# Three edits to a two-layer mixer on one core: four tiles for the rows of M, an interleaved start, and 512-column output products

## The chip, the cores and the metric

The kernel runs on one core of one Trainium2 chip, in one launch. The metric is the device time of one execution in microseconds (us). The engines are TensorE (PE, matrix products; PEld is its loading of weights), VectorE (DVE), ScalarE (ACT), GpSimd (POOL) and SyncE (SP), which issues the DMA transfers. Each engine works off its own list of instructions in order, and the order of each list is fixed when the program is built.

## The reference

Two layers, each on 512 latent tokens and 256 context tokens of 1024 channels (768 rows in all). A conditioning vector goes through the adaLN matrix (1024 x 3072) and gives a shift, a scale and a gate. Then, cut to what matters here:

```
h = rmsnorm(x, pre_g) * (1 + scale) + shift
s = split(h @ w_in)                    # 13,408 columns
ya = bidirectional RG-LRU(s)           # branch a
yb = bidirectional gated linear attention(s)   # branch b
yc = bidirectional Mamba-2 SSD(s)      # branch c, 32 heads of 64, state 128
pa, pb, pc = (ya*silu) @ w_pa, (norm(yb)*silu) @ w_pb, norm(yc*silu) @ w_pc
o  = (g0*pa + g1*pb + g2*pc) @ w_out
x  = x + gate * rmsnorm(o, post_g)
```

In branch c, within a chunk of tokens, y[t] = sum over s of cb[t,s] * exp(cum[t]-cum[s]) * x[s], plus the state's part, times exp(cum[t]), and then times the silu gate of z. cb times that exponential, masked, is the matrix M. The context runs through layer 0 in full; layer 1 needs only its states.

## The kernel before

**How products are made.** All of it is float32. A product a*b is three products of shorter numbers (fp32r): high part by high part, high by low, low by high. Whoever writes an operand for PE splits it: a copy into the high part (`hh`, `oh`, `wh`) and a subtraction for the low part (`hl`, `ol`, `wl`; L356 is the subtraction). Activations stand with channels on the partitions, as eight k tiles of 128 x 768.

**The order.** `Sched` is a list scheduler that runs when the program is built. Each piece of work is a stream (a Python generator) that yields operations, needs (events such as `("raw", 1)`: "weight tile 1 is loaded") and requests for a tile from a small ring (`Slots`). Among the streams that are free to go on, it takes the operation with the earliest modelled start; so any edit to a ring or a need can move everything behind it. Helpers emit all operations, so the profile's lines are mostly theirs: L410 matmul, L414 the half-width product with M, L419 transpose, L423 DMA, L332 activation, L373 two-operand DVE operation, L404 copy under a mask, L551 adaLN product.

**Weights.** An `Item` is 0.5 MB of weights and what is done with them. The `loader` brings items in order into a ring of two raw tiles (four in the ring that w_out has), the `splitter` splits each in two halves into `wh` and `wl` (four halves of 512 columns), and `main` runs the bodies in order. PSUM has two large tiles (`pp`, 2 x 512 columns) for projections and four small ones (`aux`).

**The start.** `start` loads eight adaLN blocks of 1 MB, ring of six, one after the other; the loads of x's six row tiles go between them (`x` stream i needs block i+1), and small parameters too. Blocks come as pairs (0 and 4, 1 and 5, ...): the pair gives shift and scale for two k tiles. `make_h_part` then makes the two k tiles for each of three pairs of row tiles (transposes, an affine step, a split). The first two items, the dt projection (96 columns) and the first x projection (128 columns), go through `acc_first`: row pairs 0 and 1 first over all k tiles, then row pair 2.

**M's rows.** `ssd_ms` makes one row of M (128 tokens x 4 heads) from two `rr` tiles: each is loaded by DMA (the cumulated sums, broadcast over the partitions), ACT adds a bias per head (four operations each), DVE merges the two under a mask, ACT takes the exponential, DVE multiplies by cb and sets the diagonal. The result stays in the first `rr` tile until PE has used it (L414, two products to a head pair); the second goes back at once. `ssd_ec` loads, per row, an `ec` tile of exp(cum); `ssd_scan` multiplies the state's products by it, adds, and `out` multiplies the sum by z's gate, which needs both z projections of the group (`gz`, L373), and only then gives the `ec` tile back. There are 80 rows.

**w_out.** Per pair of row tiles, `it_wout` runs four blocks of 256 columns by two halves of four k tiles; a body waits for both halves of its weights. A tail per block multiplies by the gate (`o`) and squares (`sq`); the last tail starts the closing normalisation, `post`.

Of the kernel before, what the change touches and what calls it, by code (L numbers as in the profile page):

```python
# [287 lines left out]
class Mixer(Sched):  # L288
# [288 lines left out]
    def ada_load(self, l, q, raws):  # L577
        for blk in ADA_BLOCKS:
            raw = yield from self.acquire(raws)
            yield from self.dma(raw, self.a["ada_w"][l][:, blk * 256:(blk + 1) * 256].rearrange("(k p) n -> p k n", p=P))  # L580
            self.first.append(raw)
            self.done.add(("adal", blk))
            yield from self.param_loads(l, q, 5)

# [22 lines left out]
    def loader(self, items):  # L607
        for i, it in enumerate(items):
            pieces, kk, nn = it.units
            if it.ring != "w":  # L610
                yield ("need", [("open", it.ring)])
            raw = yield from self.acquire(self.raws[it.ring])
            rv = raw[:, :kk * nn].rearrange("p (k n) -> p k n", k=kk)
            for c0, src in pieces:
                yield from self.dma(rv[:, :, c0:c0 + src.shape[1]], src.rearrange("(k p) n -> p k n", p=P))
            self.rawq.append((raw, rv))
            self.done.add(("raw", i))
# [71 lines left out]
    def acc_first(self, ps, us, l, rows=P):  # L689

        for pairs in ((0, 1), (2,)):
            for k in range(KT):
# [957 lines left out]
    def it_wout(self, S, pair, n, kh):  # L1650
        l = S.l
        early = n == 0 and pair == (0 if S.nc_ else 1)

        def tail(ps, n, o, x, ss):
            cs = slice(n * 256, (n + 1) * 256)
            for i in range(2):
                yield from self.tt(o[i][:, cs], ps[:, i, :256], S.gp[1 if pair == 0 else 0][:, cs], ALU.mult)
            for i in range(2):
                junk = yield from self.acquire(S.junk2_)
                yield from self.act(junk, ps[:, i, :256], AF.Square, accum=ss[i][:, n:n + 1])  # L1660
                self.free(junk)
            self.free(ps)
            if n == 3:
                self.spawn(("h", l + 1, pair), self.post(S, pair, o, x, ss), 1)
# [4 lines left out]
        def body(us):  # L1669
            if n == 0 and kh == 0:  # L1670
                o = yield from self.acquire(S.o_, 2)
                x = yield from self.acquire(S.x_in, 2)
                S.o = (o, x, [S.e_.tile([P, 4], F32, name=self.nm("ss")) for _ in range(2)])
                for i in range(2):
                    self.spawn(("xin", l, pair, i), load(i, x[i]), 2)
            if kh == 0:
                S.ops = yield from self.acquire(self.pp)
            yield ("need", [us.second])
            for i in range(2):
                out = S.ops[:, i, :256]  # L1680
                sl = slice((pair * 2 + i) * P, (pair * 2 + i + 1) * P)
                for kk in range(4):
                    k = kh * 4 + kk
                    h, lo = us.high(kk, 0, 256), us.low(kk, 0, 256)
                    yield from self.mm(out, S.mh[k][:, sl], h, k == 0, False)
                    yield from self.mm(out, S.mh[k][:, sl], lo, False, False)
                    yield from self.mm(out, S.ml[k][:, sl], h, False, k == KT - 1)
            if kh == 1:
                self.spawn(("wt", l, pair, n), tail(S.ops, n, *S.o), 0, [("gp", l), ("wt", l, pair, n - 1)] if n else [("gp", l)])
        need = [("pbr", l, 0, j) for j in range(8)] if (n, kh) == (0, 0) else []  # L1690
        return Item(("w", l, pair, n, kh), ([(0, self.a["w_out"][l][kh * 512:(kh + 1) * 512, n * 256:(n + 1) * 256])],
                                            4, 256), body, need, ring="w" if early else f"e{l}")

# [105 lines left out]
    def tail_items(self, S):  # L1799
        r = [self.it_wout(S, pr, n, kh) for pr in ((0, 1, 2) if S.nc_ else (1, 2))  # L1800
             for n in range(4) for kh in range(2)]
        return r

    def start(self, q, st, ip, src):
# [10 lines left out]
        def load(i):  # L1815
            yield from self.dma(xs[i], src(i))
            j = yield from self.acquire(junk)
            yield from self.norm_tile(ip, xs[i], j)
            self.free(j)
        for i in range(NCH):  # L1820
            self.spawn(("x", i), load(i), 0, [("adal", ADA_BLOCKS[1 + i])])
        self.alloc_h()
# [5 lines left out]
    def run(self):  # L1828
        a = self.a
        with self.tc.manual_schedule():  # L1830
# [15 lines left out]
            self.spawn(("par", 1), self.params(1, q1), 3, [("start",)])  # L1846
            self.spawn(("loader",), self.loader(items), 2, [("adaload",)])
            self.spawn(("splitter",), self.splitter(items), 2, urgent=lambda: self.ahead <= W_LOW)
# [4 lines left out]
class Layer:  # L1853
# [9 lines left out]
    def open_c(self):  # L1863
# [27 lines left out]
        self.sf_ = Slots(k, c, "sf", 2, [P, 256])  # L1891
        self.rr_ = Slots(k, c, "rr", 3, [P, 4, P])
        self.ec_ = Slots(k, c, "ec", 3, [P, 2, 2, P])

# [56 lines left out]
    def open_e(self):  # L1951
# [5 lines left out]
        self.junk_ = Slots(k, e, "junk", 1, [P, D])  # L1957
        self.junk2_ = Slots(k, e, "sq", 2, [P, 256])
        ring = f"e{self.l}"
# [48 lines left out]
```

## Time and profile before

| | |
|---|---|
| median of 3 runs | 2750.03 us (2747.54 to 2751.88) |
| the profiled execution | 2755.44 us, of it the span 2753.6 |
| mean granted clock of PE | 0.991 |
| busy: PE, DVE, ACT, POOL | 2667.7, 2104.9, 1222.8, 297.5 us |
| share of the span | 97%, 76%, 44%, 11% |
| DMA | 329.37 MB, 120 GB/s |

The span runs from the first instruction to the last; the profiled execution is 1.84 us longer. Busy times are sums over instructions. A timeline's line gives its start, its duration, the operation and how many ran in a row, and in brackets how long the engine had idled before and for whom. A clock of 1.00 is full speed, and 0.61 over a stretch is a mean over full and half speed.

### The profile page before, as it was taken

The numbers are of one execution on the slowest core, as the hardware profiler recorded it, in microseconds if no ns is written. First come the engines' busy times: TensorE is split into PE (matmuls) and PEld (weight loads), VectorE is DVE, ScalarE is ACT, GpSimd is POOL, SyncE is SP. The second block draws the span as 40 slices with busy tenths as digits, with TensorE's granted clock in tenths as the row PEclk, the third lists the DMA queues.
The fourth block names the chain that finished last, engine by engine and source line by source line (L and its number), as shares of the span: only waits on it lengthen the run. The fifth ranks groups of instructions, "written<-read, shape, count | busy, mean of one in ns | idle before, by whom it ended". The sixth has DMA issues, their size and how long they took to land. (4 is left out here: it accounts for less than half of the span.)

```text
span 2753.6 us, 42894 instructions
## 1 busy us (share of the span) xinstructions
PE 2667.7 (97%) x16294; PEld 2298.6 (83%) x16294; DVE 2104.9 (76%) x3990; ACT 1222.8 (44%) x2350; POOL 297.5 (11%) x398
## 2 busy tenths in 40 slices
PE   7999899999999999999999999999999999999898
PEld 5888788888889888888889987878888888888787
DVE  5788979898665653668956879999997766568987
ACT  4445555454413331326722555556453333246742
POOL 1021112122000000000000203122120000000000
PEclk9999899999999999999999999999999999999999
DMA  6353444435352222462155635344354532243255
GB/s 211 91 142 81 123 107 118 113 94 137 103 184 73 68 67 81 136 195 62 52 164 181 205 88 132 95 123 112 104 134 129 173 84 78 73 140 112 63 157 199
DMA packets 491966, 329.37 MB, mean 120 GB/s; under 512 B 19812, under 2 KB 466864, under 8 KB 491760
## 3 DMA queue, kind: packets, MB, share of 16 engines
q1 hardware_dynamic: 491760, 326.63, 42.1%
q8 instruction: 128, 2.10, 0.3%
q14 instruction: 78, 0.64, 0.1%
HBM read 294.12 MB, written 32.45 MB: 119 GB/s over the span
## 5 line engine op out<-in xcount | busy, mean ns | idle before, releaser
L410 PE MATMUL pp<-hh,wh 128*128 128x256 f32 (+2 forms) x2624 | 760.8, 352 | 13.0 <-DVE r L380 4.6
L410 PE MATMUL pp<-hl,wh 128*128 128x256 f32 (+2 forms) x2624 | 765.3, 353 | 0.2 <-DVE hl L356 0.2
L410 PE MATMUL pp<-hh,wl 128*128 128x256 f32 (+2 forms) x2624 | 763.0, 352 | 0.0
L410 PEld LDWEIGHTS pp<-hh,wh 128*128 128x128 f32 (+1 forms) x2624 | 487.3, 189 | 78.9 <-issue 9.6
L410 PEld LDWEIGHTS pp<-hh,wl 128*128 128x128 f32 (+1 forms) x2624 | 488.2, 189 | 60.0 <-issue 0.5
L410 PEld LDWEIGHTS pp<-hl,wh 128*128 128x128 f32 (+1 forms) x2624 | 487.4, 189 | 59.4 <-issue 1.2
L356 DVE TENSOR_TENSOR wl<-raw,wh 128x512 fp32r<-128x512 f32 (+1 forms) x628 | 442.6, 708 | 46.9 <-ACT wh L341 14.7
L342 DVE CAST wh<-raw 128x512 fp32r<-128x512 f32 (+1 forms) x364 | 159.4, 438 | 300.4 <-PE pp L410 282.6
L332 ACT ACTIVATE rr<-rr,tokp 128x128 f32<-128x128 f32 x640 | 202.7, 390 | 157.4 <-DMA rr<-cumd 156.9
L341 ACT CAST wh<-raw 128x512 fp32r<-128x512 f32 (+1 forms) x264 | 161.8, 617 | 233.2 <-PE pp L410 195.2
L375 POOL TENSOR_TENSOR xw<-xt,tokp 128x256 f32<-128x256 f32 x157 | 133.5, 850 | 529.3 <-DVE xwl L356 349.5
L332 ACT ACTIVATE r<-pp 128x768 f32<-128x768 f32 (+1 forms) x112 | 78.3, 700 | 187.1 <-PE pp L410 186.9
L410 PE MATMUL pp<-oh,wh 128*128 128x512 f32 (+1 forms) x384 | 119.3, 362 | 0.8 <-DVE gz L380 0.8
L410 PE MATMUL pp<-oh,wl 128*128 128x512 f32 (+1 forms) x384 | 117.9, 360 | 0.0
L410 PE MATMUL pp<-ol,wh 128*128 128x512 f32 (+1 forms) x384 | 117.9, 359 | 0.0
L410 PE MATMUL pp<-yh,wh 128*128 128x512 f32 (+1 forms) x384 | 116.1, 356 | 0.0
L410 PE MATMUL pp<-yh,wl 128*128 128x512 f32 (+1 forms) x384 | 115.6, 355 | 0.0
L410 PE MATMUL pp<-yl,wh 128*128 128x512 f32 (+1 forms) x384 | 115.4, 355 | 0.0
L410 PE MATMUL pp<-wh,hl 128*128 128x256 f32 x384 | 109.1, 284 | 0.0
L332 ACT ACT_TABLE_LOAD x79 | 101.4, 1283 | 17.1 <-PE pp L410 10.9
L410 PE MATMUL pp<-wl,hh 128*128 128x256 f32 x384 | 108.7, 283 | 0.0
L410 PE MATMUL pp<-wh,hh 128*128 128x256 f32 x384 | 108.7, 283 | 0.0
(275 smaller groups left out, 4887.9 us busy)
## 6 DMA issues: line engine op xcount, KB each, us to landing
raw<-in_w_in_dram SPq DMA_DIRECT2D x208, 512.0 KB
rr<-cumd SPq DMA_DIRECT2D x160, 256.0 KB
ec<-ecumd SPq DMA_DIRECT2D x160, 128.0 KB
raw<-in_w_out_dram SPq DMA_DIRECT2D x40, 512.0 KB
raw<-in_w_pc_dram SPq DMA_DIRECT2D x32, 512.0 KB
raw<-in_ada_w_dram SPq DMA_DIRECT2D x32, 512.0 KB
ada<-in_ada_w_dram SPq DMA_DIRECT2D x8, 1024.0 KB
raw<-in_w_pb_dram SPq DMA_DIRECT2D x16, 512.0 KB
```

The lines of the kernel that those rows point to most:

```text
L332: self.nc.scalar.activation(out, in_, func, **kw)
L341: yield from self.any_op([("ACT", self.acost(n, in_), lambda: self.nc.scalar.copy(out, in_)), ("DVE", self.vcost(n, in_, True), lambda: se ...
L342: ("DVE", self.vcost(n, in_, True), lambda: self.nc.vector.tensor_copy(out, in_))],
L356: ways = [("DVE", self.vcost(n, a), lambda: self.nc.vector.tensor_tensor(out, a, b, ALU.subtract))]
L375: ways.append(("POOL", self.gcost(n), lambda: self.nc.gpsimd.tensor_tensor(out, a, b, op)))
L410: lambda: self.nc.tensor.matmul(out, lhsT, rhs, start=start, stop=stop))
```

## The change

1. **The start.** The small parameters come after the second adaLN block, all six row tiles of x right behind them, then the weights of the first two items, and only then adaLN blocks three to eight. The third item's weights wait for the last block. `acc_first` in layer 0 goes k tile by k tile over the three row pairs, so a body can go on as each pair of blocks frees two k tiles.
2. **M's rows.** The ring `rr` has four tiles, and the ring `ec` two, each 2 KB a partition.
3. **w_out.** An item is two k tiles by 512 columns: 480 products of 512 columns instead of 960 of 256. The body begins with its first half, gives it back, and then waits for the second. Tails handle 512 columns.

```
@@ ada_load
-        for blk in ADA_BLOCKS:
+        for i, blk in enumerate(ADA_BLOCKS):
             raw = yield from self.acquire(raws)
+            if i == 2:
+                yield ("need", [("xl", t) for t in range(NCH)] + [("raw", 1)])
...
-            yield from self.param_loads(l, q, 5)
+            if i:
+                yield from self.param_loads(l, q)
@@ loader
+            if i == 2:
+                yield ("need", [("adaload",)])
@@ acc_first
+        if l == 0:
+            for k in range(KT):
+                for p in range(3):
+                    yield ("need", [("hk", l, p, k)] + ([us.second] if k >= KT // 2 else []))
+                    out = self.rows_of(ps[:rows, 1, :], l, p) if p else ps[:rows, 0, 512 - TC:]
+                    h, lo = us.high(k, 0, rows), us.low(k, 0, rows)
+                    for i, (w, x) in enumerate(((h, self.hh[k]), (h, self.hl[k]), (lo, self.hh[k]))):
+
+                        yield from self.mm(out, w, self.rows_of(x[:, TC:], l, p) if p else x[:, :TC],
+                                           k == 0 and i == 0 and p < 2, k == KT - 1 and i == 2 and p != 1)
+            return
@@ it_wout
-                yield from self.tt(o[i][:, cs], ps[:, i, :256], S.gp[1 if pair == 0 else 0][:, cs], ALU.mult)
+                yield from self.tt(o[i][:, cs], ps[:, i, :], S.gp[1 if pair == 0 else 0][:, cs], ALU.mult)
...
-            yield ("need", [us.second])
-            for i in range(2):
-                out = S.ops[:, i, :256]
-                sl = slice((pair * 2 + i) * P, (pair * 2 + i + 1) * P)
-                for kk in range(4):
-                    k = kh * 4 + kk
-                    h, lo = us.high(kk, 0, 256), us.low(kk, 0, 256)
+            for kk in range(2):
+                k = kh * 2 + kk
+                if kk:
+                    us.release(0)
+                    yield ("need", [us.second])
+                h, lo = us.high(kk, 0, 512), us.low(kk, 0, 512)
+                for i in range(2):
+                    out = S.ops[:, i, :]
+                    sl = slice((pair * 2 + i) * P, (pair * 2 + i + 1) * P)
                     yield from self.mm(out, S.mh[k][:, sl], h, k == 0, False)
                     yield from self.mm(out, S.mh[k][:, sl], lo, False, False)
                     yield from self.mm(out, S.ml[k][:, sl], h, False, k == KT - 1)
...
-        return Item(("w", l, pair, n, kh), ([(0, self.a["w_out"][l][kh * 512:(kh + 1) * 512, n * 256:(n + 1) * 256])],
-                                            4, 256), body, need, ring="w" if early else f"e{l}")
+        return Item(("w", l, pair, n, kh), ([(0, self.a["w_out"][l][kh * 256:(kh + 1) * 256, n * 512:(n + 1) * 512])],
+                                            2, 512), body, need, ring="w" if early else f"e{l}")
@@ start
             yield from self.dma(xs[i], src(i))
+            self.done.add(("xl", i))
...
-            self.spawn(("x", i), load(i), 0, [("adal", ADA_BLOCKS[1 + i])])
+            self.spawn(("x", i), load(i), 0, [("rows", 0)])
@@ run
-            self.spawn(("loader",), self.loader(items), 2, [("adaload",)])
+            self.spawn(("loader",), self.loader(items), 1, [("xl", t) for t in range(NCH)])
@@ open_c
-        self.rr_ = Slots(k, c, "rr", 3, [P, 4, P])
-        self.ec_ = Slots(k, c, "ec", 3, [P, 2, 2, P])
+        self.rr_ = Slots(k, c, "rr", 4, [P, 4, P])
+        self.ec_ = Slots(k, c, "ec", 2, [P, 2, 2, P])
```

Left out are a few lines that follow from it: the slices and counts in `it_wout` and `tail_items` (two blocks of 512 by four items), and the sizes of `sq` (512) and `ss` (2).

SP's list at the start, from the fourth adaLN block (`ada_174`) on, before:

```order
L423 DMA ada_174<-in_ada_w_dram 128x8x256
L423 DMA x_106<-in_x_dram 128x1024
L423 DMA ada_178<-in_ada_w_dram 128x8x256
L423 DMA x_107<-in_x_dram 128x1024
L423 DMA ada_181<-in_ada_w_dram 128x8x256
L423 DMA x_108<-in_x_dram 128x1024
L423 DMA ada_184<-in_ada_w_dram 128x8x256
L423 DMA x_109<-in_x_dram 128x1024
L423 DMA ada_197<-in_ada_w_dram 128x8x256
L423 DMA raw_202<-in_w_in_dram 128x8x64
L423 DMA raw_202<-in_w_in_dram 128x8x32
L423 DMA raw_208<-in_w_in_dram 128x8x128
```

and now, behind the row tile `x_107`:

```order
L423 DMA x_108<-in_x_dram 128x1024
L423 DMA x_109<-in_x_dram 128x1024
L423 DMA raw_178<-in_w_in_dram 128x8x64
L423 DMA raw_178<-in_w_in_dram 128x8x32
L423 DMA raw_188<-in_w_in_dram 128x8x128
L423 DMA ada_159<-in_ada_w_dram 128x8x256
L423 DMA ada_203<-in_ada_w_dram 128x8x256
L423 DMA ada_214<-in_ada_w_dram 128x8x256
L423 DMA ada_224<-in_ada_w_dram 128x8x256
L423 DMA ada_231<-in_ada_w_dram 128x8x256
L423 DMA ada_237<-in_ada_w_dram 128x8x256
```

The two items' weights (`raw`: 64 and 32 columns for dt, 128 for x) moved from behind the last adaLN block to ahead of the third (`ada_159`), and x's loads no longer alternate with the blocks.

PE's list at the start, at the last adaLN block's product (`ada_197`), before; `pp_459` is the dt projection, and its first product is the last row:

```order
L551 MATMUL aux_420<-ada_197,cfull 32x256 x8
L419 MATMUL aux_441<-ident,x_109 128x128
L419 MATMUL aux_442<-ident,x_109 128x128
L419 MATMUL aux_420<-ident,r_453 128x128 x2
L419 MATMUL aux_478<-ident,x_104 128x128
L419 MATMUL aux_478<-ident,x_105 128x128
L419 MATMUL aux_479<-ident,x_104 128x128
L419 MATMUL aux_479<-ident,x_105 128x128
L419 MATMUL aux_480<-ident,x_106 128x128
L419 MATMUL aux_480<-ident,x_107 128x128
L410 MATMUL pp_459<-hh_110,wh_209 96x256 x2
```

and now, around the product of the third block (`ada_203`), with `pp_313` the dt and `pp_322` the x projection, and the number behind `hh` counting the k tiles from 110:

```order
L419 MATMUL aux_192<-ident,r_347 128x128 x2
L410 MATMUL pp_313<-hh_110,wh_189 96x256
L410 MATMUL pp_322<-hh_110,wh_297 128x256
L410 MATMUL pp_313<-hl_118,wh_189 96x256
L410 MATMUL pp_313<-hh_110,wl_190 96x256
L410 MATMUL pp_313<-hh_111,wh_189 96x256
L410 MATMUL pp_322<-hl_118,wh_297 128x256
L410 MATMUL pp_322<-hh_110,wl_298 128x256
L410 MATMUL pp_322<-hh_111,wh_297 128x256
L551 MATMUL aux_346<-ada_203,cfull 32x256 x8
```

Products of both projections now stand among the adaLN blocks' own, with k tiles 110 and 111 ahead of the third block, where before the first product of a projection stood behind the last.

PE's list in layer 0 where group 0 of branch c ends (about 290 us before); `pp_3120` is a projection, `pp_3365` the first product with w_pc, `xt_2448` the x of group 1's first half, whose six rows of M are the 13th to 18th, before:

```order
L410 MATMUL pp_3120<-hh_117,wl_2974 128x512
L414 MATMUL aux_3231<-rr_3104,xt_2448 64x128 x4
L410 MATMUL aux_3232<-ct_2875,sb_2924 128x128 x2
L414 MATMUL aux_3285<-rr_3230,xt_2448 64x128 x4
L410 MATMUL aux_3286<-ct_2875,sf_3165 128x128 x2
L410 MATMUL aux_3319<-xwh_3310,btok_2872 128x256
L410 MATMUL aux_3319<-xwl_3311,btok_2872 128x256
L410 MATMUL aux_3319<-xwh_3310,btokl_2873 128x256
L414 MATMUL aux_3347<-rr_3284,xt_2448 64x128 x4
L410 MATMUL aux_3348<-ct_2875,sf_3210 128x128 x2
L410 MATMUL aux_3348<-ct_2875,sb_3124 128x128 x2
L410 MATMUL pp_3365<-oh_3244,wh_3045 128x256
```

and now, at the first of the same three rows of M (`xt_2563` is the same x):

```order
L410 MATMUL pp_3044<-hh_116,wl_2915 128x512
L414 MATMUL aux_3158<-rr_2970,xt_2563 64x128 x4
L410 MATMUL aux_3159<-ct_2801,sb_2840 128x128
L419 MATMUL aux_3136<-ident,r_3045 128x128 x4
L410 MATMUL aux_3159<-ct_2801,sb_2840 128x128
L410 MATMUL pp_3044<-hh_117,wh_2914 128x256
L410 MATMUL pp_3044<-hh_117,wh_2914 128x512
L410 MATMUL aux_3172<-xwh_3162,btok_2782 128x256
L410 MATMUL pp_3044<-hl_125,wh_2914 128x256
L410 MATMUL pp_3044<-hl_125,wh_2914 128x512
L410 MATMUL pp_3044<-hh_117,wl_2915 128x256
L410 MATMUL pp_3044<-hh_117,wl_2915 128x512
```

Before, three products with M stood in eight rows, with only small products between. Now the first of them is at row 1324 of PE's list and the next three at 1354, 1414 and 1441, with the rest of `pp_3044`, one more projection and the first two products with w_pc between them. On DVE's list the last low part of group 0 that w_pc needs (`ol`, from `gz`) is row 488, and was row 491. Over the whole program PE's list is 13,593 rows and was 14,027, DVE's 3891 and 3888, ACT's 1779 and 1809, POOL's 387 and 403.

## Rows read from the trace of the kernel before

**Rows 1.** Page, part 1: busy us (share of the span) x instructions
```profile
PE 2667.7 (97%) x16294; PEld 2298.6 (83%) x16294; DVE 2104.9 (76%) x3990; ACT 1222.8 (44%) x2350; POOL 297.5 (11%) x398
```

**Rows 2.** Page, part 2: busy tenths of PE in 40 slices
```profile
PE   7999899999999999999999999999999999999898
```

**Rows 3.** Windows: us, busy us of each engine, PE's clock, DMA share, GB/s
```profile
3.00:36.00 33.00, 20.10 (x138) 9.34 (x138) 13.35 (x50) 12.01 (x25) 4.53 (x11) 0.90 1.07 354
36.00:41.00 5.00, 3.29 (x39) 1.46 (x38) 4.70 (x13) 3.52 (x9) 0.95 (x2) 1.00 0.88 179
...
65.00:250.00 185.00, 183.69 (x1148) 157.84 (x1147) 147.33 (x295) 85.34 (x189) 28.39 (x35) 1.00 0.44 114
...
290.00:312.00 22.00, 11.06 (x57) 8.46 (x57) 21.58 (x38) 10.27 (x26) 2.40 (x4) 0.61 0.35 96
...
1495.00:1572.00 77.00, 73.59 (x606) 72.44 (x605) 66.11 (x128) 41.04 (x105) 13.40 (x18) 1.00 0.65 209
1760.00:1820.00 60.00, 57.41 (x310) 44.67 (x310) 57.17 (x115) 34.08 (x82) 15.01 (x18) 1.00 0.45 118
```

**Rows 4.** Timeline of PE, 0:110: start, us, line, operation [idle before <-releaser]
```profile
39.50 1.07 PE L551 MATMUL aux<-ada,cfull 128*32 128x256 f32 x16
...
42.73 0.48 PE L410 MATMUL pp<-hh,wh 128*96 128x256 f32 x2
...
64.55 0.28 PE L410 MATMUL pp<-hh,wl 128*128 128x256 f32 x1
```

**Rows 5.** Timeline of DVE, 39:46 us
```profile
44.35 0.54 DVE L350 TENSOR_SCALAR r<-aux,asc,mod 128x256 f32<-128x256 f32 x1
44.93 0.29 DVE L342 CAST hh<-r 128x256 fp32r<-128x256 f32 x1
45.26 0.42 DVE L356 TENSOR_TENSOR hl<-r,hh 128x256 fp32r<-128x256 f32 x1
```

**Rows 6.** Timeline of PE, 2689.7:2708.1, w_pa (512 columns), then w_out
```profile
2689.75 0.39 PE L410 MATMUL pp<-yh,wh 128*128 128x512 f32 x1
...
2694.96 0.39 PE L410 MATMUL pp<-yh,wl 128*128 128x512 f32 x1
...
2703.00 0.28 PE L410 MATMUL pp<-wh,ml 128*128 128x256 f32 x1
...
2707.80 0.28 PE L410 MATMUL pp<-wh,mh 128*128 128x256 f32 x1
```

**Rows 7.** Groups by form, whole run, then 1495:1572: busy, mean ns | idle, releaser
```profile
L410 PE MATMUL pp<-wl,mh 128*128 128x256 f32 x320 | 91.8, 287 | 4.3 <-DVE wl L356 4.3
...
L410 PE MATMUL pp<-wl,mh 128*128 128x256 f32 x191 | 55.1, 289 | 3.4 <-DVE wl L356 3.4
```

**Rows 8.** Groups by form, whole run: the tails of PSUM pieces
```profile
L373 DVE TENSOR_TENSOR ec<-aux,ec 128x512 f32<-128x512 f32 x64 | 43.9, 686 | 18.2 <-PE aux L410 17.9
...
L332 ACT ACTIVATE r<-pp 128x512 f32<-128x512 f32 x56 | 33.1, 592 | 63.8 <-PE pp L410 63.8
...
L373 DVE TENSOR_TENSOR o<-pp,gp 128x256 f32<-128x256 f32 x40 | 15.2, 417 | 4.1 <-PE pp L410 4.1
...
L332 ACT ACTIVATE sq<-pp 128x256 f32<-128x256 f32 x40 | 15.0, 380 | 20.4 <-DVE o L373 20.4
```

**Rows 9.** Timeline of PE, 255:330 us: products with M's rows
```profile
298.60 1.12 PE L414 MATMUL aux<-rr,xt 128*64 128x128 f32 x8 [5.44 <-DVE rr L404]
...
307.08 1.12 PE L414 MATMUL aux<-rr,xt 128*64 128x128 f32 x8 [4.16 <-DVE rr L404]
```

**Rows 10.** Groups by form, whole run: M's rows on ACT and PE
```profile
L332 ACT ACTIVATE rr<-rr,tokp 128x128 f32<-128x128 f32 x640 | 202.7, 390 | 157.4 <-DMA rr<-cumd 156.9
...
L414 PE MATMUL aux<-rr,xt 128*64 128x128 f32 x640 | 55.0, 289 | 14.0 <-DVE rr L404 13.8
```

**Rows 11.** SP's waits: line, awaited: us in total, times, longest us
```profile
SPq L423 <- DVE wl L356: 1344.1, 240, 21.2
...
SPq L423 <- DVE gz L373: 85.0, 24, 7.7
```

## What was predicted

> **What bounds the kernel now.** I read the page first. TensorE (PE) is busy for 97% of the span, VectorE (DVE) for 76%, and nothing else is near [rows 1]. The 40 slices say where the missing 3% lie: the first slice, the fifth and the last are the ones where PE drops most [rows 2]. So a change can win in two ways only: by taking time from PE's own instructions, or by closing one of the holes. The table by stretch puts numbers on the holes [rows 3]. From 65 to 250 us PE works 183.69 of 185 us. From 290 to 312 us it works 11.06 of 22 at a mean clock of 0.61, while DVE works 21.58 of the 22. In layer 0's w_out stretch, from 1495 to 1572 us, PE works 73.59 of 77. So each part of the change gets its price from one stretch: the start, the stretch around 300 us, and w_out.
>
> The sum is made against the profiled execution, 2755.44 us (span 2753.6 and 1.84 around it). The median of the timed runs is 2750.03, 5.4 less; I take the gain off both alike.
>
> **The start.** PE takes up the last adaLN block at 39.50 us and the first projection at 42.73; the last matmul of the x projection, the second, starts at 64.55 [rows 4]. After the last block PE therefore has 25 us to go, and 144 matmuls of 0.12 us (2 projections, 8 k tiles, 3 terms, 3 pieces), 17.3 us, are nearly all in them. The change loads all of x and the two projections' weights ahead of adaLN blocks 3 to 8, and takes the products k tile by k tile. A pair of blocks frees two k tiles, so three quarters of the matmuls (108, 13 us) can run before the last pair is there.
>
> What it costs: the two weight tiles, 0.92 MB, go ahead of the last blocks. At the start's 354 GB/s that is 2.6 us, at the 179 GB/s of the stretch in which these tiles move now, 5.1 [rows 3]. That stretch holds short pieces and SP's waits too, so I take 4. The DMA engines are full until 36 us, so the last block lands at about 40 instead of 36, and PE can start on it near 40.5. From there I copy today's chain [rows 4, 5]: the block's matmuls start at 39.50, and the first piece that waits for its scale is begun at 44.35, 4.8 us later. Then come the last two k tiles for three row pairs, six pieces: ACT takes three (as now, it shares them), DVE does 3 x (0.54 + 0.29 + 0.42) and three more low parts of 0.42, 5.0 us. About a dozen matmuls are left, 1.4 us. 40.5 + 4.8 + 5.0 + 1.4 = 51.7 against 64.7: 13 us less. The clock at the start is 0.5 for a part of the time (mean 0.90 from 3 to 36 us, with PE at work 20.10 of 33 us), and PE's work will now come in more pieces between waits; I leave 1 us for that and take **-12 us**. Bounds: -14 if the weights pass at full rate and the clock is up; -5.5 if all 108 matmuls run at the lower clock (26 us, where there are 19 between 22 and 41, so 7 run over). The next items need nothing new: their weights are split when the dt projection gives its parts back, with the x projection's last matmuls as cover. Without that cover it would be one split, 0.4 + 0.7 us.
>
> **w_out.** 960 matmuls of 256 columns [rows 7] become 480 of 512, with the same number of columns in all. The steady intervals are in one stretch: 24 matmuls of 512 columns start 5.21 us apart from first to last, 0.2265 each; 41 of 256 columns 4.80 us, 0.120 each [rows 6]. Two short ones cost 0.240, one long one 0.2265: 13.5 ns less, 480 times, **-6.5 us** (3.9 in layer 0, 2.6 in layer 1). The weights are still 2 halves of 512 columns an item, so DVE's and ACT's splitting is the same; DVE works 66.11 of 77 us there, so PE stays the bound.
>
> The Trainium skill, TensorE: Matmul & The Clock Gate, section "Wait — 56ns, not 53.3ns?", says that a warm matmul costs its columns at 2.4 GHz and a fixed 2.5 ns. By that, 480 matmuls fewer would give 1.2 us. The slope agrees here (106.5 ns for 256 columns), the constant doesn't: the rows leave 13.5 ns.
>
> PE also waits 3.4 us for DVE's low parts in layer 0's w_out [rows 7]. The new body needs its second half later and gives the first back sooner, so some of it may go; but DVE's work at a pair's end stays. -0.5 (bounds 0 and -3.4). On the other side the last piece's tail now handles 512 columns: two multiplies and two squares of 256 columns (0.417 and 0.380 us) [rows 8] become two of 0.686 and 0.592, the means of like 512-column operations that read PSUM. That is 0.54 + 0.42, **+1.0 us** at the very end, where nothing hides it. At the layer boundary the same microsecond falls beside layer 1's first projections, which PE has in hand there; if that cover were gone it would be 1 us more.
>
> **A fourth tile for M's rows, and one less for ec.** Around 300 us PE waits 5.44 and 4.16 us for two rows of M that follow each other [rows 9], 9.6 of its 13.8 us of such waits [rows 10]. The order shows why: three rows stand with almost nothing between them. With the clock at 0.5 for most of the stretch, the 11.06 us of work are worth some 7, so the hole costs 15 us. ACT waits for the rows' DMA, 156.9 us over the run [rows 10]: that is what a fourth tile takes away. In the new order the first rows stand earlier, and between the three rows stand projections and the first w_pc products.
>
> But DVE is full there (21.58 of 22), and the w_pc products need four low parts from DVE, the last of them as far down DVE's order as before (row 488, was 491). PE would then wait for these instead. What can help is only that DVE did some rows' work earlier, when it had time (147.33 of 185 us from 65 to 250). I take a third of the hole, **-5 us**. Bounds: -15, all of it, and +4, since DVE's order has a few operations more that POOL did (16 rows fewer there). In layer 1 DVE is full while M's rows are made (57.17 of 60 us from 1760) [rows 3], so a shorter ACT wait buys nothing there; I put **+1** for POOL's lost share.
>
> Sum: -12 - 6.5 - 0.5 + 1 - 5 + 1 = **-22 us**, 2733.4 in the profile's terms, **2728 us** for the median.
>
> **The rivals.**
> 1. DVE holds the hole as it is, and the additional DVE work shows: 0 and +3 for M's rows instead of -5 and +1. Sum -15, 2735. For: DVE's 21.58 of 22 us. Against: the new order brings DVE work forward. It includes the case that the fourth tile does nothing, because two tiles for ec let the scan get only two rows ahead.
> 2. The start is bound elsewhere (clock, DVE's splits between the pieces): -5.5. Sum -15.5, 2734.5.
> 3. The skill's constant holds for the new matmuls (TensorE: Matmul & The Clock Gate): w_out gives -1.2 instead of -6.5. As a mechanism of this kernel: what is saved per matmul is 2.5 ns. Sum -17, 2733. The rows speak against it.
> 4. Everything closes: the whole hole (-15), and the w_out waits (-3.4). Sum -36, 2714; with a gain in the other waits for rows (13.8 - 9.6 = 4.2 us) some 2710.
> 5. Slower: ec with two tiles blocks SP. SP's queue is in order and also carries the weights. It already waits 24 times, 85.0 us in all, for the last multiply that frees an ec tile [rows 11]; with two tiles the load of a row waits for the row two before it. It decides from the point where such a wait is longer than what SP waits anyway for a weight tile (1344.1 us in 240 waits, 5.6 each), since up to there the weights would not have been fetched sooner. A row lasts 8.5 us (298.60 to 307.08) [rows 9]. If 30 of the 80 rows then hold the weights up by 1.5 us beyond that, it is +45: sum +23, 2773. Against: the last multiply comes soon after a row's products, except for the rows that wait for their gates.
>
> **How the numbers follow.** Forecast 0.52 (its own range 2719 to 2737), rival 1 0.19, rival 2 0.08, rival 3 0.05, rival 4 0.10, rival 5 0.06. A measurement can tell 0.2% (5.5 us) from no change, so faster is below 2744.5. Rivals 1 to 3 end near 2734, and with misses of 10 us some 0.08 of them and of the forecast fall within 0.2%. Faster 0.86, same 0.08, slower 0.06. The range for 8 in 10 reaches from rival 4 to the weak side of rivals 1 and 2: 2709 to 2744.
>
> **What would show it.** Start: the x projection's last matmul near 52 us, with matmuls of both projections from about 25 us on. w_out: 480 matmuls of 512 columns 0.2265 us apart; 0.2380 would be the skill's rule. M's rows: no run of three waits near 285 us, the ACT wait for rows well under 157 us, and in their place waits of w_pc's products for `ol`. The end: about 1 us more from the last matmul to the end. Wrong, if the hole near 300 us is closed altogether, if PE's waits for weights grow, or if PE's idle time comes back in layer 1.

## The result, and the profile after

The changed kernel takes 2731.82 us (median of 4 runs, 2728.5 to 2734.77), the kernel before 2749.7 beside it: a ratio of 0.9929, 95% interval 0.9916 to 0.9942. The forecast was 2728 with a range from 2709 to 2744. The total is right, and by luck: its terms are not, and their errors cancelled. That is what the rest is about.

The page of the changed kernel, parts 1 and 2, and its windows (length, busy us of PE, PEld, DVE, ACT and POOL, clock, DMA share, GB/s):

```profile
PE 2655.9 (97%) x15814; PEld 2268.5 (83%) x15814; DVE 2113.0 (77%) x3993; ACT 1211.4 (44%) x2301; POOL 283.6 (10%) x382
...
PE   7999999999999999999999999999999999999898
```

```profile
8.50:13.50 5.00, 3.15 (x23) 1.07 (x20) 0.00 (x0) 0.74 (x2) 0.00 (x0) 1.00 0.34 86
...
31.00:45.00 14.00, 13.34 (x128) 9.71 (x120) 7.74 (x27) 6.09 (x14) 0.00 (x0) 1.00 1.11 342
...
290.00:312.00 22.00, 20.42 (x136) 16.90 (x135) 20.96 (x45) 10.40 (x26) 3.15 (x4) 1.00 0.46 126
1475.00:1547.00 72.00, 69.42 (x320) 56.38 (x318) 64.04 (x115) 37.68 (x79) 12.95 (x16) 1.00 0.66 222
```

PE's slices have lost the dip in the fifth [rows 2]. From 290 to 312 us PE now works 20.42 of 22 us at full clock, where it worked 11.06 at 0.61 [rows 3], though DVE is as full as it was (20.96, was 21.58). Layer 0's w_out, moved up by some 20 us, takes 72 us with PE at work for 69.42 [rows 3].

Where the time went, from the two traces. The stages end at the same matmuls in both kernels, and a time is that of a matmul's start:

| stage | before, us | after, us | difference |
|---|---|---|---|
| to the last matmul of the first two projections | 64.55 | 60.49 | -4.06 |
| from there to layer 0's last w_pc product | 743.61 | 727.03 | -16.58 |
| to the first w_out product | 686.81 | 687.23 | +0.42 |
| layer 0's w_out, first to last start | 77.28 | 72.14 | -5.14 |
| to layer 1's last w_pc product | 601.71 | 605.34 | +3.63 |
| to its first w_out product | 521.22 | 521.38 | +0.16 |
| layer 1's w_out | 48.58 | 44.47 | -4.11 |
| from the last matmul to the end | 9.79 | 10.66 | +0.87 |
| span | 2753.6 | 2728.7 | -24.8 |

The profiled execution of before (2755.44) lies 5.7 us above the median of its runs, that of after (2730.46) 1.4 below its own; so 24.8 here are 18 in the medians.

### The profile page after: what moved, and what is told of

It is laid out like the page before. It is cut to its first block, busy times and chain, and to the rows that moved or that the text cites. A ratio compares the mean times of both kernels' runs of the same rounds, so it can differ in the third digit from the quotient of the medians.

```text
span 2728.7 us, 41794 instructions
## 1 busy us (share of the span) xinstructions
PE 2655.9 (97%) x15814; PEld 2268.5 (83%) x15814; DVE 2113.0 (77%) x3993; ACT 1211.4 (44%) x2301; POOL 283.6 (10%) x382
## 4 chain that ended last, share of the span: by engine, by line
PE 68%; DVE 22%; DMA 3%; issue 3%; ACT 2%; SPq 1%; POOL 0%; DVEq 0%; POOLq 0%; ACTq 0%
PE pp L410 56%; PE aux L410 8%; DVE wl L356 3%; DVE r L380 2%; PE aux L419 2%; DVE rr L404 2%; DMA rr<-cumd 1%; DVE ec L373 1%; PE aux L414 1%; DVE w L373 1%; DVE xa L380 1%; PE aux L551 1%; DVE sb L373 1%; DVE gz L380 1%; DVE wh L342 1%
## 5 line engine op out<-in xcount | busy, mean ns | idle before, releaser
L342 DVE CAST wh<-raw 128x512 fp32r<-128x512 f32 x357 | 155.0, 434 | 294.0 <-PE pp L410 278.0
L332 ACT ACTIVATE rr<-rr,tokp 128x128 f32<-128x128 f32 x640 | 201.8, 390 | 129.6 <-DMA rr<-cumd 127.2
L332 ACT ACT_TABLE_LOAD x77 | 98.8, 1283 | 12.8 <-PE pp L410 10.6
```

The source lines that it names most:

```text
L332: self.nc.scalar.activation(out, in_, func, **kw)
L342: ("DVE", self.vcost(n, in_, True), lambda: self.nc.vector.tensor_copy(out, in_))],
```

## The experiments

All ran with the kernel before beside them. The last column is the ratio's distance from 1, in us of 2749. Each trace is one execution, and executions of one kernel differ by up to 12 us, so a stage's difference of a few us means little by itself. "Layer 1" is in what follows the time from layer 0's first w_out product to layer 1's last w_pc product.

| kernel | median, us | ratio and interval | us |
|---|---|---|---|
| start alone | 2759.94 | 1.0033 (1.0022 to 1.0045) | +9 |
| rings alone | 2742.28 | 0.9969 (0.9958 to 0.9980) | -9 |
| w_out alone | 2747.11 | 0.9987 (0.9977 to 0.9996) | -4 |
| start and rings | 2733.09 | 0.9940 (0.9926 to 0.9953) | -16 |
| rings and w_out | 2744.12 | 0.9976 (0.9967 to 0.9985) | -7 |
| all three (the change) | 2731.82 | 0.9929 (0.9916 to 0.9942) | -20 |
| start alone, model nudged | 2746.23 | 0.9989 (0.9981 to 0.9998) | -3 |
| before, model nudged | 2751.91 | 1.0010 (1.0001 to 1.0019) | +3 |
| two ec tiles alone | 2745.22 | 0.9985 (0.9976 to 0.9994) | -4 |
| the change, w_out new in layer 1 only | 2733.62 | 0.9942 (0.9929 to 0.9955) | -16 |
| the change, small rows between the loads | 2728.19 | 0.9921 (0.9907 to 0.9934) | -22 |
| that, new rings in layer 0 only | 2735.78 | 0.9952 (0.9937 to 0.9966) | -13 |
| that, model nudged | 2720.55 | 0.9892 (0.9877 to 0.9907) | -30 |

### One part at a time

Each of the three takes one part of the diff above and leaves the others as before. The start alone (the edits in `ada_load`, `loader`, `acc_first`, `start` and `run`):

> The kernel before with the new start alone (loads, k by k first products); rings and w_out as before. Theory, from the two traces: the last matmul of the first two projections comes 4.1 us earlier (60.5 us instead of 64.6), not 13, because PE works without a pause from 33 us on; the three rows of M near 290 us still stand together in PE's order, so their hole stays: -4 us, 2746. Rival: the earlier start is also what closed the hole near 300 us (-15 or more, 2734 or less).

It came out slower than before. Both theories missed: the start closes no hole (the waits of 5.4 and 4.3 us for M's rows stand where they stood), and the time is 14 us over the first one. Its trace has layer 1 at 683.9 us, where before has 679.0.

The rings alone:

```
-        self.rr_ = Slots(k, c, "rr", 3, [P, 4, P])
-        self.ec_ = Slots(k, c, "ec", 3, [P, 2, 2, P])
+        self.rr_ = Slots(k, c, "rr", 4, [P, 4, P])
+        self.ec_ = Slots(k, c, "ec", 2, [P, 2, 2, P])
```

> The kernel before with four rr tiles and two ec tiles alone. Theory: this alone spreads the rows of M in PE's order and closes the hole near 300 us, idle time and half clock together: -16 in layer 0, some 4 given back in layer 1, 2737. Rival 1 (DVE holds the hole, the start closed it): 2748 or more. Rival 2 (two ec tiles block the loads): slower than before.

The first theory holds in layer 0: from the first two projections to the last w_pc product 724.9 us, where the kernels with the old rings have 743.6 (before) and 742.6 (w_out alone), 18 less. But layer 1 takes 685.9 us, 7 more than before. What is left is 7 to 9.

The w_out alone (the edits in `it_wout` and `tail_items`):

> The kernel before with the 512-column w_out alone. Theory: 480 matmuls 0.2265 us apart instead of 960 0.120 apart, 5.2 us less in layer 0's stretch and 4.1 in layer 1's, 0.9 more after the last matmul: -8, 2741. Rival (2.5 ns fixed cost of a matmul): -1, 2748.

Half of the theory's 8 or less: by the time alone the rival's -1 is as near. Its mechanism is not there, though. In the trace w_out takes 72.24 and 44.42 us, as the theory has it; what is missing was lost at the layer boundary (below).

The three parts alone add up to -3 us; together they give -20. So the parts act on each other.

### Why they don't add

PE's lists show a candidate. In layer 1 the rows of M stand 20 rows of PE's list and more apart in the kernel before. With the start alone three distances are 9, 9 and 9 rows, with the rings alone 9 and 9; with all three parts the smallest is 12. I call rows 9 apart a bunch. The scheduler places them by its modelled clock, and any edit ahead of layer 1 shifts that.

The change without its w_out:

> The changed kernel with the old 256-column w_out: the new start and the new rings. Alone the start gave +10 us and the rings -7. Theory: what made the start alone slower is in layer 1, where the scheduler's modelled clock had put three rows of M together in PE's order (9 rows apart, three times); with the rings they stand 23, 21 and 12 rows apart again, so the loss goes away and the two together give about what the changed kernel has less its w_out, 2735. Rival: the parts simply add, 2752.

2733: the theory to within its interval, and far from the sum of the parts. The change without its start:

> The changed kernel with the old start: the new rings and the new w_out. Theory: in layer 1's PE order three rows of M stand together here (9, 9, 23 rows apart) as with the rings alone, so layer 1 is 5 to 6 us longer than in the changed kernel, and the sum is that of the two parts, 2739. Rival: the start itself is worth little (it has given back all but 1 us by 100 us), so without it the time is that of the changed kernel, 2732.

2744, 12 us over the whole change, 5 more than I had expected; layer 1 takes 692.2 us here, 677.5 in the whole change. The first two projections end 4.2 us apart in the two, but at the 300th projection product, near 98 us, 1.7 us are left, and 1.1 at layer 0's last w_pc product. So the start's worth in this change is, nearly all of it, that layer 1 comes out in another order.

To vary the order and nothing else, a number of the scheduler's model was changed by 17 ns:

```
-ACT_LOAD = 1283
+ACT_LOAD = 1300
```

> The kernel before with the new start alone, and one number of the scheduler's model changed: a table load of ACT is modelled with 1300 ns instead of 1283. Nothing else is edited; the order of the lists shifts, and in layer 1 the three rows of M no longer stand together (23, 25, 37 rows apart instead of 9, 9, 9), while those near 290 us in layer 0 still do (2 and 5). Theory: the start alone loses its 10 us in layer 1 by that order only: now 2749 to 2752. Rival: something in the new start itself costs 10 us (SP's list, the loader's place): 2760 again.

The start alone loses all of its 9 us and 3 more: 12 us by the ratios, 14 by the medians, between two programs that differ in an estimate. That is 3 us below the theory's range. Layer 1 goes from 683.9 to 666.1 us, and the stage ahead of layer 0's last w_pc product from 744.8 to 749.4, so the nudge shifts more than the bunch. The same number of the model, now 1305 for 1283, in the kernel before, where no bunch comes or goes:

> The kernel before, with that one number of the scheduler's model changed (1305 instead of 1283) and nothing else; the hole near 300 us keeps its order (2 and 5 rows), and no rows of M stand close in layer 1, before as now. Theory: where no bunch comes or goes, the number itself is worth little: 2744 to 2752. Rival: the nudge itself speeds layer 1 by 10 us, 2739.

+3, at the upper end of the theory, so a higher number is not faster by itself. It isn't neutral either: the stage in layer 0 takes 748.4 us (743.6 before) and layer 1 675.4 (679.0). A pair made for the question, on the best start (below), with the new rings in layer 0 alone:

```
-        self.rr_ = Slots(k, c, "rr", 4, [P, 4, P])
-        self.ec_ = Slots(k, c, "ec", 2, [P, 2, 2, P])
+        self.rr_ = Slots(k, c, "rr", 4 if self.nc_ else 3, [P, 4, P])
+        self.ec_ = Slots(k, c, "ec", 2 if self.nc_ else 3, [P, 2, 2, P])
```

> The kernel with the small rows between the loads (2728), with the new rings in layer 0 alone and three and three tiles in layer 1. In layer 1's PE order three rows of M stand 9, 9 and 9 rows apart. Theory: these bunched rows cost layer 1 what they cost with the start alone, 8 to 12 us over that kernel: 2736 to 2740. Rival: the place of the rows in the order of PE is not what makes the difference in layer 1: within 3 us of 2728.

and the same with 1305:

> The same as the kernel with the new rings in layer 0 alone, with one number of the scheduler's model changed (a table load of ACT modelled with 1305 ns instead of 1283), by which no two rows of M in layer 1 stand closer than 20 rows. Theory: layer 1 takes what it took in the nudged kernel with the start alone, 666 us from the first w_out product to the last of w_pc where the kernel with the rows between has 674: 2719. Rival: 2728 or more.

2735.8 and 2720.6, within 2 us of the theory, with 681.9 and 666.6 us in layer 1: the 15 us are that stage. Most of them arise at the bunch. Counted in projection products on PE from layer 0's first w_out product, the first kernel is 3.2 us ahead of the second at the 5,550th, 14.7 behind at the 5,575th, and 10.2 behind at the 5,725th, where it has settled: 13 us. The start alone against its nudged twin makes the same step, from 2.7 ahead to 10.7 behind. Here are the products with M's rows at the bunch, on PE, and the window from 1740 to 1785 us, in the first of the two:

```profile
1758.21 1.12 PE L414 MATMUL aux<-rr,xt 128*64 128x128 f32 x8 [2.55 <-DVE sf L373]
...
1765.24 1.12 PE L414 MATMUL aux<-rr,xt 128*64 128x128 f32 x8 [1.86 <-DVE rr L404]
...
1773.50 1.12 PE L414 MATMUL aux<-rr,xt 128*64 128x128 f32 x8 [1.99 <-DVE rr L404]
```

```profile
1740.00:1785.00 45.00, 35.23 (x178) 28.42 (x177) 41.72 (x86) 20.68 (x56) 13.09 (x15) 0.85 0.46 127
```

and in the second:

```profile
1765.89 0.66 PE L414 MATMUL aux<-rr,xt 128*64 128x128 f32 x8
...
1772.09 0.66 PE L414 MATMUL aux<-rr,xt 128*64 128x128 f32 x8
...
1780.83 0.66 PE L414 MATMUL aux<-rr,xt 128*64 128x128 f32 x8
```

```profile
1740.00:1785.00 45.00, 44.23 (x247) 34.81 (x246) 43.76 (x88) 26.67 (x65) 14.30 (x14) 1.00 0.42 118
```

The rows come at the same pace in both, 6 to 9 us apart, with DVE nearly full (41.72 and 43.76 us of 45). In the second PE has projections to do between them and works 44.23 of 45 us; in the first it waits ahead of each (the first time for the state `sf`, not for the row), works 35.23, and the mean granted clock of the window is 0.85. That is the hole near 300 us [rows 9] in another place. The second is also the fastest kernel of this study: 1.1% under before, and its interval lies below that of the change.

The bunch is not all that the order does. Six kernels have no two rows of M closer than 20 in layer 1, and they take 666 to 679 us there, the kernel before the longest. Where that spread arises is open.

### Which ring closes the hole in layer 0

```
-        self.ec_ = Slots(k, c, "ec", 3, [P, 2, 2, P])
+        self.ec_ = Slots(k, c, "ec", 2, [P, 2, 2, P])
```

> The kernel before with two ec tiles instead of three, and nothing else (three rr tiles). Theory: two ec tiles cost nothing by themselves, and the hole near 300 us stays where it was, since the rows of M there still stand 40, 5 and 26 rows apart in PE's order (2 and 5 before): within 5 us of before, and waits for M's rows near 300 us of 5 us and more. Rival 1: two tiles block SP's queue, 5 us and more slower than before. Rival 2: the gain of the rings comes from the ec side: the hole closes, 2742.

The time is within 5 us of before, as the theory has it, but neither the theory nor a rival has the hole right: the order moves a little and with it a part of the hole. The stage that holds it takes 738.1 us (743.6 before, 724.9 with both rings), and the longest wait for a row of M is 2.51 us (this execution lies 4.7 us under the median of its runs):

```profile
299.68 1.12 PE L414 MATMUL aux<-rr,xt 128*64 128x128 f32 x8 [2.51 <-DVE rr L404]
```

So two ec tiles cost no time, though SP waits longer for them (120.6 us in 30 waits, 85.0 in 24 before [rows 11]), and the fourth rr tile is needed for the rest. Four rr with three ec tiles don't fit into the memory, so the fourth tile by itself is not measured.

### w_out in layer 0

The change with layer 0's w_out as before (a copy of the old `it_wout` for layer 0):

> The changed kernel, with layer 0's w_out at 256 columns as before and layer 1's at 512. Theory: in layer 0 PE gets through w_out 5 us sooner and then waits 2.4 us for layer 1's first h, which comes from the last tail and the normalisation behind it, so of the 5.1 us some 1.5 remain: 1.5 us slower than the changed kernel, 2733. Rival: layer 0's shorter w_out counts in full, 2736 to 2737.

1.8 us slower by the medians, 3.6 by the ratios, and the intervals overlap: the times don't decide it. The traces do. Counted from the first w_out product, the 4,801st projection product on PE, which lies in layer 1, starts after 90.16 to 90.25 us in seven of the eight kernels with 256 columns in layer 0 (91.73 in the eighth), and after 89.40 to 89.73 in five of the six with 512 (88.25 in the sixth). Of the 5.1 us some 0.6 are left. In between stands a wait that before has not. PE in the changed kernel, DVE beside it, PE's window behind the wait, and PE's first product of layer 1 in the kernel before:

```profile
1549.72 0.50 PE L410 MATMUL pp<-hh,wh 128*128 128x256 f32 x2 [2.44 <-DVE wh L342]
```

```profile
1549.25 0.42 DVE L342 CAST wh<-raw 128x512 fp32r<-128x512 f32 x1
...
1550.31 1.28 DVE L373 TENSOR_TENSOR o<-pp,gp 128x512 f32<-128x512 f32 x2
```

```profile
1550.90:1554.30 3.40, 3.40 (x19) 3.40 (x18) 2.46 (x6) 1.26 (x4) 1.54 (x3) 0.51 0.61 150
```

```profile
1572.38 0.40 PE L410 MATMUL pp<-hh,wh 128*96 128x256 f32 x2
```

The theory has the wait's length right and its cause wrong. What comes last is not h but the high part of layer 1's first weight tile (`wh`), which DVE makes at 1549.25; layer 0's last tail (`o`, at 1550.31) and the normalisation come after the wait. The split stands late in DVE's list, behind the pieces of layer 1's h, and DVE works 10.76 us of the 11 from 1539 on. The wait takes 2.4 of the 5.1 us. Right behind it the granted clock is at half for 3.4 us, which takes most of what else is lost: the kernel with 88.25 us has a wait of 2.35 us there and no such fall.

### The start

SP in the changed kernel (start, duration, operation, how many):

```profile
5.58 0.31 SPq L423 DMA_DIRECT2D r<-in_conv_a_b_dram  x1
6.87 0.32 SPq L423 DMA_DIRECT2D r<-in_lru_br_dram  x1
9.87 0.32 SPq L423 DMA_DIRECT2D r<-in_lru_bi_dram  x1
...
12.14 0.83 SPq L423 DMA_DIRECT2D x<-in_ctx_dram  x2
...
15.01 7.02 SPq L423 DMA_DIRECT2D raw<-in_w_in_dram  x3
22.08 13.79 SPq L423 DMA_DIRECT2D ada<-in_ada_w_dram  x6
```

The row loads at 6.87 and 9.87 us are the eighth issues behind the first and the second adaLN block, and each goes out only when that block has landed. SP's waits in the first 24 us say the same (us in total, times, longest):

```profile
SPq L423 <- DMA ada<-in_ada_w_dram: 3.6, 2, 2.7
```

In the program's list every issue waits for the one eight places ahead of it. So the small rows wait for the two large blocks, x goes out only from 12.14 us, and from 8.5 to 13.5 us the DMA engines are busy for 0.34 of the time, at 86 GB/s (the window above). The rows were put between the loads:

```
-            if i:
-                yield from self.param_loads(l, q)
+            if i < 2:
+                for n, x in ((5, None),) if i == 0 else ((4, 1), (4, 3)):
+                    if x is not None:
+                        yield ("need", [("xl", x)])
+                    yield from self.param_loads(l, q, n)
+                    self.done.add(("pr", x))
...
-            self.spawn(("x", i), load(i), 0, [("rows", 0)])
+            self.spawn(("x", i), load(i), 0, [("adal", 4)] if i < 2 else [("pr", 1 if i < 4 else 3)])
```

> The changed kernel, with the small parameter rows loaded among the large loads (five behind the first adaLN block, four behind the second row tile of x, four behind the fourth) instead of all before x. Theory: in the changed kernel SP stands at the row loads until the two adaLN blocks have landed, since an issue waits for the transfer eight issues earlier, and the DMA engines run nearly empty from 8.5 to 13.5 us; with the rows in between they stay full, the blocks and x come 4 us earlier, and the first two projections end near 56.5 us: 2728 where the changed kernel has 2732. Rival: PE is full from 33 us on and sets the end of the first projections whatever the loads do: within 1 us of the changed kernel.

```profile
8.50:13.50 5.00, 2.81 (x25) 0.77 (x17) 0.00 (x0) 1.73 (x3) 0.69 (x2) 1.00 1.05 396
...
31.00:45.00 14.00, 13.73 (x139) 10.27 (x139) 7.73 (x27) 5.38 (x13) 0.00 (x0) 1.00 1.05 310
```

The DMA engines are full from 8.5 us on (396 GB/s), and the first two projections end at 58.75 us, 1.7 earlier, not 4: between the theory and the rival, since PE is full from 31 us on (13.73 of 14, the second line) in both. By the times it is 2 to 4 us better than the change, with overlapping intervals, so they don't tell it from the change.

## Why the prediction was right, and where not

**The start (-12, bounds -14 to -5.5).** Two steps failed: that three quarters of the matmuls (108) "can run before the last pair is there", and that "the next items need nothing new". On PE the mechanism is there, in the rows of the changed kernel: products from 25 us on, the third adaLN block at 29.72, the last at 48.57, the dt projection's last product, the x projection's, and a new wait:

```profile
25.03 0.56 PE L410 MATMUL pp<-hh,wh 128*96 128x256 f32 x1
...
29.72 1.94 PE L551 MATMUL aux<-ada,cfull 128*32 128x256 f32 x16 [0.23 <-DMA ada<-in_ada_w_dram]
...
48.57 1.07 PE L551 MATMUL aux<-ada,cfull 128*32 128x256 f32 x16
...
59.17 0.28 PE L410 MATMUL pp<-hh,wl 128*96 128x256 f32 x1
...
60.49 0.28 PE L410 MATMUL pp<-hh,wl 128*128 128x256 f32 x1
...
72.04 0.59 PE L410 MATMUL pp<-hh,wh 128*128 128x256 f32 x2 [2.25 <-DVE r L380]
```

First, the last block is taken up at 48.57, not 40.5: x and the blocks went out late, for the reason above, and from 31 to 45 us PE works 13.34 of 14 (the window above), so it is bound by its own work and no longer by the blocks. By then 66 of the 144 products have started, not 108. The 78 others are left, not a dozen, and PE works 12.13 of 12.13 us from there to the end of both projections. The clock was lower than I read, too. The trace's record of it begins at 21.8 us before and at 32.0 after, and the view counts what lies ahead as 1.00, so the 0.90 of [rows 3] is too high. An adaLN block's product takes 1.94 us at 29.72 and 1.07 at 48.57, so the first products, from 25 to 32 us, ran at the lower level.

Second, taken k tile by k tile, the two projections end together. The dt projection was done 7 us ahead of the other before and now is 1.3 ahead (59.17 and 60.49): its end has moved back, from 55.8 to 57.7 in the six kernels with the old start to 59.2 to 61.0 in five with the new one. Behind it hangs a chain on ACT and DVE, which the x projection's convolution stands behind on DVE, and that frees the PSUM tile PE waits for at 72.04. DVE in the kernel with the rings alone (old start), and in the changed one:

```profile
61.47 0.95 DVE L373 TENSOR_TENSOR gz<-gz,gz 64x768 f32<-64x768 f32 x1 [3.31 <-ACT gz L332]
...
63.11 3.82 DVE L400 TENSOR_TENSOR_SCAN gz<-ones,gz 32x128 f32<-32x128 f32 x9
66.86 2.78 DVE L380 SCALAR_TENSOR_TENSOR r<-pp,p,r 128x504 f32<-128x504 f32 x5
```

```profile
65.32 0.95 DVE L373 TENSOR_TENSOR gz<-gz,gz 64x768 f32<-64x768 f32 x1 [2.54 <-ACT gz L332]
...
66.96 1.70 DVE L400 TENSOR_TENSOR_SCAN gz<-ones,gz 32x128 f32<-32x128 f32 x4
68.68 3.21 DVE L380 SCALAR_TENSOR_TENSOR r<-pp,p,r 128x504 f32<-128x504 f32 x6
```

The chain begins 3.9 us later (65.32 for 61.47), and the convolution (`r<-pp`) 1.8 (68.68 for 66.86). And behind the wait at 72.04 the clock falls:

```profile
73.00:76.40 3.40, 3.40 (x12) 2.92 (x11) 3.30 (x9) 0.00 (x0) 0.00 (x0) 0.50 0.02 5
```

Before it is 1.00 in the same stretch. At half speed for 3.4 us PE loses 1.7 us. At the 300th projection product the six kernels with the old start stand at 96.26 to 99.02 us and five with the new one at 97.32 to 99.19. The gain of this part is nil; with the rows in between it is 95.77. The rival "the start is bound elsewhere" had the right side but still 5.5 us too many.

**M's rows (-5, bounds -15 to +4).** The mis-sized term: -18 in layer 0 (727.0 and 724.9 us in the change and with the rings alone, 742.6 to 744.8 in the three kernels with the old rings and the model as it was). That goes beyond the bound of the whole hole. Set beside each other by the columns that PE has done, the kernel before loses 14 us to the rings alone at the hole itself, close to the 15 I had put for it, and the rest in smaller steps elsewhere in the stage. My own sign of being wrong, "if the hole near 300 us is closed altogether", has come. The argument against it was that DVE is full there. It is nearly full now, too (20.96 of 22), and it did not matter: what counted was whether PE has other work between the rows. The rows stand at row 1324, 1354, 1414 and 1441 of PE's list, and in the trace they come 6 to 13 us apart without a wait; what took the hole's place are 1.1 us for the high part that w_pc needs, as I had expected of `ol`:

```profile
281.31 0.66 PE L414 MATMUL aux<-rr,xt 128*64 128x128 f32 x8
...
293.47 0.62 PE L410 MATMUL pp<-oh,wh 128*128 128x256 f32 x2 [1.10 <-DVE oh L342]
294.02 0.66 PE L414 MATMUL aux<-rr,xt 128*64 128x128 f32 x8
...
300.67 0.66 PE L414 MATMUL aux<-rr,xt 128*64 128x128 f32 x8
```

The order with its projections between the rows was in front of me, and I priced DVE's share instead of PE's.

**Layer 1 (+1).** A term of the wrong kind. No run sets POOL's share apart; what the runs show is the stage's order, which makes 666 to 692 us of the same work. The change got 677.5 where before had 679.0, by chance of the model. In the six kernels that have the new rings in layer 1 some rows of M stand 9 or 12 apart there (mean 681 us), in six of the eight with three rr tiles none closer than 20 (675 for the eight); the fastest kernel uses that.

**w_out (-6.5 - 0.5 + 1).** The price of a matmul is right (PE, after; 54 rows, 53 intervals):

```profile
2706.07 0.39 PE L410 MATMUL pp<-wh,mh 128*128 128x512 f32 x1
...
2718.08 0.39 PE L410 MATMUL pp<-wh,ml 128*128 128x512 f32 x1
```

12.01 us in 53 intervals, 0.2266 each, for 0.2265 forecast. By the Trainium skill's fixed 2.5 ns (TensorE: Matmul & The Clock Gate, section "Wait — 56ns, not 53.3ns?") two of the old 0.120 us would have become 0.2375, which the prediction has as 0.2380, and the page's own figure for 512 columns is 0.2157. The rows bear out neither. The tails, too, are as priced, 0.684 and 0.595 us, and the end is 0.87 us longer. The step that failed is "PE stays the bound", with the projections that "PE has in hand there": DVE's 66.11 of 77 us is a mean over the stretch, and at its end DVE is full. There PE waits 2.4 us for DVE's split of layer 1's first weights, and the clock falls behind the wait. Of layer 0's 5.1 us 0.6 remain. In layer 1 it is -3.3 (47.8, the mean of seven kernels with 256 columns, to 44.5), less the 0.87 at the end. All told about -3, where -6 was forecast; alone it measured -2.5 to -3.6. By form, after:

```profile
L332 ACT ACTIVATE rr<-rr,tokp 128x128 f32<-128x128 f32 x640 | 201.8, 390 | 129.6 <-DMA rr<-cumd 127.2 <-PE pp L410 2.2
...
L410 PE MATMUL pp<-wl,mh 128*128 128x512 f32 x160 | 63.1, 394 | 3.4 <-DVE wl L356 3.4
...
L414 PE MATMUL aux<-rr,xt 128*64 128x128 f32 x640 | 54.7, 286 | 3.4 <-DVE rr L404 3.2
...
L373 DVE TENSOR_TENSOR o<-pp,gp 128x512 f32<-128x512 f32 x20 | 12.9, 684 | 5.1 <-PE pp L410 5.1
...
L332 ACT ACTIVATE sq<-pp 128x512 f32<-128x512 f32 x20 | 11.8, 595 | 20.6 <-DVE o L373 20.6
```

ACT's wait for the rows' DMA is down to 127.2 us from 156.9 [rows 10], and PE's for M's rows to 3.2 from 13.8; PE's for weights are 3.4, were 4.3 [rows 7].

**The sum.** -12, -6, -5 and +1 came out as about 0, -3, -18 and, in this order of layer 1, 0. The errors cancelled, so the total was right by luck. Of the rivals, the slower one (two ec tiles block SP) is refuted by the kernel with two ec tiles alone, "DVE holds the hole" by the rings alone, and the Trainium skill's constant by the 0.2266 us. "Everything closes" had the hole right and the w_out waits wrong (3.4 us remain).

## What to carry to other kernels

Where an engine's order is fixed ahead, look at what the waiting engine can do between two slow deliveries before you price the deliverer: the same pace of rows cost 13 to 14 us where they stood together and next to nothing where projections stood between. Where a model makes that order, test an edit beside a null edit of the model, for a dozen us hung on an estimate changed by 17 ns, more than any of the three parts gave alone; and time the parts alone as well as together. An end that moves up counts only if it is the end that somebody waits for.

## What the runs showed of the hardware that was not expected

In this program a DMA issue of SP waits for the transfer eight issues earlier, so 13 small loads behind two of 1 MB held the queue for 3.6 us and left the DMA engines at 86 GB/s for 5 us; with the small loads between large ones it is 396. And the clock of TensorE falls in a bunch of three waits of 1.9 to 2.6 us (0.85 over 45 us), which adds to what the waits themselves cost. A single wait can be enough: in the changed kernel PE waits 2.25 us before 72.04 and 2.44 before 1549.72, and behind each the granted clock is at half (0.50 and 0.51) for 3.4 us. It is not always so: the same wait at the layer boundary, 2.35 us, has no such fall in the fastest kernel.
